# Low halves of a hybrid block's mixer weights: a negated copy on ScalarE and an accumulating transfer in place of a GpSimd subtraction

## The chip, the core and the metric

The kernel runs on one core of a Trainium2 chip. A core has five engines with a queue of instructions each: TensorE (PE, with its weight loads shown apart as PEld), VectorE (DVE), ScalarE (ACT), GpSimd (POOL) and SyncE (SP, which here only issues transfers). Each engine runs its own queue in order and waits for the others at semaphores. Tiles lie in on-chip memory with 128 partitions, sums of matmuls in banks of their own. The metric is the device time of one execution in microseconds (us), less being better.

## The reference

Two layers of a backbone over 256 latent tokens and 256 context tokens, width 1024, all in fp32. Every layer is a half-step SwiGLU, a token mixer with four branches, and another half-step SwiGLU. Of the mixer, what matters here is that everything starts from one wide projection and ends in merges:

```python
def token_mixer(h, hc, rope, p, ctx_out):
    (ca, cg, lx, lg, gqkv, gz, ga, gb, aq, ak, av, gates) = split_in(h @ p['w_in'])
    ...                                   # the same for the context: hc @ p['w_in']
    y_conv = conformer_conv(ca, cg, p)    # depthwise convolution, width 31
    y_lru, y_lru_c = rglru_branch(...)    # gated linear recurrence, both directions
    y_gdn, y_gdn_c = gdn_branch(...)      # chunked gated DeltaNet, both directions
    y_att = window_attention(...)
    def merge(y_a, y_b, y_c, y_d, gate_cols):
        gt = jax.nn.sigmoid(gate_cols).reshape(gate_cols.shape[:-1] + (N_BRANCH, D))
        mrg = gt[..., 0, :] * (y_a @ p['proj_conv'])
        ...                               # the three other branches likewise
        return mrg @ p['w_out']
```

In the second layer the context stream is needed only as far as the latent tokens read it, so most of its projections take 256 columns (tokens) and not 512.

## The kernel before

**Split products.** TensorE multiplies in a rounded 32-bit format (fp32r). To keep fp32 accuracy each operand is split into a rounded high half and a low half, the difference between the raw value and the high half, and `mm3` (lines 379 to 381) makes three products: high weights by high activations, high by low, low by high. All weights come from memory in pieces of 128 x 1024 (512 KB), called chunks here. One chunk feeds 24 matmuls where activations stand as 512 or 256 columns.

**A chunk** is made in `chunk` (line 98). SyncE loads it into a raw tile `wr` (two buffers), ScalarE writes the rounded half `wh` (line 120, three buffers, or a longer-lived slot F, Y, B or G), and DVE or GpSimd subtracts it from the raw tile into `wl` (line 121, three buffers). A raw buffer is free for the next load when that subtraction has read it.

**Which engine subtracts** is taken from the string `self.lo`, letter by letter, by the running number of the chunk: "D" is DVE, "P" GpSimd. The FFNs set "DDP" or "D". In the mixers a table `ORDER` holds one letter for each step of work; its capital letters P, D and X set `self.lo` by the table `LO` to "P", to "DP" (turn about) and to "D". After that table `mixer` sets "DP" in the first layer and "D" in the second, for the merges of two branches and the fetch of `wo` (the table `TAIL`, where an X sets "D").

**What sets the order.** A scheduler places the instructions on the engines by priority and by its own estimate of durations, so a change of one operation moves others. The transfers are issued by SyncE in one queue: a load that waits for its raw buffer holds up everything behind it, among it the loads `gt<-gsp` (lines 818 and 822) which feed the steps of the DeltaNet scan, and the stores `gsp<-G`.

**Other names that the prediction uses.** Line 1107 is the width-31 convolution on DVE: 240 multiply-adds `C<-C,vec`, each with two operands in on-chip memory. Lines 858 to 893 are the steps of the scan, which alternate between TensorE, DVE and GpSimd (line 868 decays the state). Line 1049 is the short convolution of the recurrence. Line 1294 adds a gated product into the merge tile on GpSimd. Line 132 loads an identity matrix at the start; it is the only transfer that GpSimd issues. `wab` is a small weight of 64 KB that ScalarE's queue loads.

Of the kernel before, what the change touches and what calls it, by code (L numbers as in the profile page):

```python
# [12 lines left out]
F32 = mybir.dt.float32  # L13
# [3 lines left out]
ALU = mybir.AluOpType  # L17
P = 128
D = 1024
# [13 lines left out]
    0, 124, 128, 132, 136, 168, 176, 184, 192, 200, 296, 298, 300, 301, 309)  # L33
NEG = -1e30
N_CH = 16
LO = {"P": "P", "D": "DP", "X": "D"}
ORDER = (
    "eggePgegeggXgeggggggPgegggvggvggvggvgggggggaabgggabggzabababzabababllllggababababzababgllablglzbvvvvvccccvvccvccssssssssPssssssDmmllllmmllllsmmmmsmmmmmmmm",
    "gPggggeeeggecgggcgeggggeggccgvgvggvvggggccgagggggbaabgzggggvggabzvabgccggvabbabazbvvvvvzssssslssssssslllllsPssmmlllllsmmmllllmlmmmmmmmmmm",
# [10 lines left out]
class Net:  # L50
# [46 lines left out]

    def chunk(self, src, at=None, raw=None):
        nc = self.nc
        pool_lo = self.lo[self.n_ck % len(self.lo)] == "P"  # L100
        self.n_ck += 1
        if raw is None:
            raw = self.sb.tile([P, 1024], F32, tag="wr", bufs=2, name="wr")
            nc.sync.dma_start(raw, src)
        elif isinstance(raw, str):
            raw = self.slot(raw, name="raw")[:, :1024]
            nc.sync.dma_start(raw, src)
        if at == "G":
            hi, lo = ([self.G(F32R) for _ in range(2)] for _ in range(2))
            parts = [(hi[k], lo[k], raw[:, k * 512:(k + 1) * 512]) for k in range(2)]  # L110
        else:
            if at:
                w = self.slot(at, F32R, name="w" + at)
                hi, lo = w[:, :1024], w[:, 1024:]
            else:
                hi = self.sb.tile([P, 1024], F32R, tag="wh", bufs=3, name="wh")
                lo = self.sb.tile([P, 1024], F32R, tag="wl", bufs=3, name="wl")
            parts = [(hi, lo, raw)]
        for h, l, r in parts:
            nc.scalar.copy(h, r)  # L120
            (nc.gpsimd if pool_lo else nc.vector).tensor_sub(l, r, h.bitcast(F32))  # L121
        return hi, lo

    def split(self, hi, lo, src, pool_lo=True):
# [280 lines left out]
    def ffn(self, l, f, j, tiles, H, fill, after, start=None):  # L405
# [9 lines left out]
        def two(src, at=(None, None)):  # L415
            if lat:
                return self.pair(src, "Y", at)
            return [chunk(src[a], at[a]) for a in range(2)]

        for fi, (m0, m1) in enumerate(F_SPLIT):  # L420
# [48 lines left out]
            if fi < len(F_SPLIT) - 1:  # L469
                for dh in range(2):  # L470
                    ps = {t: self.ps("px" if t == 3 else "pm") for t in tiles}
                    ws = []
                    for i in range(n):
                        i0 = m0 // 2 + i
                        if i == n - 1 and not i % 2:
                            ws.append(chunk(src[dh][i]))
                        elif not i % 2:
                            ws += two(self.t["f2"][l, f, dh, i0:i0 + 2])
                        w = ws[i]
                        for t in tiles:  # L480
                            self.down_mm(ps[t], hid, t, n, i, w)
                        if fill and i % 2:
                            fill.pop(0)()
                    for t in tiles:
                        self.resid(t, dh, ps[t], ALPHA if fi == 0 else 1.0)
            else:
                while fill:
                    fill.pop(0)()
                ws = [[chunk(src[dh][i], at=DOWN_AT[dh][i]) for i in range(n)] for dh in range(2)]


# [41 lines left out]
        else:  # L533
            nc.vector.tensor_add(x, x, t1)

# [1 line left out]

    def z_mm(self, ps, w, H, c):
        for k in range(KD):
# [759 lines left out]
    def mixer(self, l, H, last, after):  # L1299
        nc = self.nc  # L1300
        tiles = (2, 3) if last else (0, 1, 2, 3)
        c = slice(256, 512) if last else slice(0, 512)
        self.vec = self.sb.tile([P, V_N], F32, tag="vec", bufs=1, name="vec")
        with self.tc.issue_after(self.mark):
            nc.scalar.dma_start(self.vec, self.t["vec"][l])
        self.l, self.inv = l, None
        self.ysp = [self.dr.tile([P, 4, 512], F32, tag=f"ysp{b}", bufs=1, name="ysp") for b in range(4)]
        for s in range(2):
            if not (last and s == 0):
                nc.sync.dma_start(self.xspill[s], self.x[s])  # L1310
        self.z_head(l, H, [Z_GK + h for h in range(4)] + [Z_AK if last else Z_GQ])
        S, extra = self.att_z(l, H, last)
        self.conv_init()
        self.gdn_init()
        st = dict(
            g=self.gdn(l, H, last), v=self.gdn_values(l, H, last), s=self.gdn_scan(last),
            e=(f() for f in extra), a=self.att(self.att_scores, S, tiles),
            b=self.att(self.att_values, S, tiles), z=(self.gdn_z(l, H, last, h) for h in range(4)),
            c=(x for i in range(4) for x in self.conv(l, H, last, i)), l=self.lru(l, H, last), m=self.merges(l, H, last, c))
        ws = {}  # L1320
        self.emit(st, ORDER[l], "gvezabclsm")
        self.lo = "D" if last else "DP"
        y = [None, None]
        if last:
            mh = [a.rearrange("p (k t) -> p k t", k=KD) for a in (self.F(F32R), self.F(F32R))]
            spots = SPOT
        else:
            spots = ("F", "F", "F", "F", "F", "G", "G", None)
        self.ju = self.T

        def fetch(n0, n1):
            for n in range(n0, n1):
                ws[n] = self.chunk(self.t["wo"][l, n // 4, n % 4], at=spots[n])

        def conv_out():
            y[0] = self.new_y()
            self.conv_norm(last, y[0])
            yield

        def gdn_out():  # L1340
            y[1] = self.new_y()
            for t in tiles:
                self.gdn_out(t, y[1])
                yield

        done = [0] * 4

        def merged(i):
            done[i] += 1
            if last and done[i] == 2:  # L1350
                self.mh_split(mh, i, c)

        def merge_conv():
            for i in range(4):
                yield from self.merge(l, 0, y[0], H, last, False, i, lambda: merged(i))

        def merge_gdn():
            for i in range(4):
                yield from self.merge(l, 2, y[1], H, last, False, i, lambda: merged(i))

        def fetches():
            for i in range(4 if last else 7):
                fetch(i, i + 1)
                yield

        self.emit(dict(n=conv_out(), o=gdn_out(), c=merge_conv(), g=merge_gdn(), f=fetches()), TAIL[l], "nocgf")
        if not last:
            mh = self.new_h()
            for i in range(4):
                self.mh_split(mh, i, c)  # L1370
        self.x = [None, None]
        for s in range(2):
            if not (last and s == 0):
                self.x[s] = self.Y(name="x")
                nc.sync.dma_start(self.x[s], self.xspill[s])
        self.gate_rows(l, 1, 0.5, (1,) if last else (0, 1))
        self.norm_rows(l, 1)
        fetch(4 if last else 7, 8)

        def mm(t, dh, sums):  # L1380
            ps = self.ps()
            with self.hold():
                for i in range(4):
                    self.wo_mm(ps, mh, t - 2 if last else t, i, ws[4 * dh + i])
            self.resid(t, dh, ps, ALPHA, sums)

        self.out_loop(tiles, mm, after)

    def emit(self, streams, order, rest):
        for ch in order:  # L1390
            if ch in LO:
                self.lo = LO[ch]
            else:
# [165 lines left out]
```

## Time and profile before

| | us |
|---|---|
| median of 3 runs | 2820.98 (2819.75 to 2821.17) |
| span of the profiled execution | 2816.3 |
| PE busy | 2593.8 (92%) |
| DVE busy | 1955.0 (69%) |
| ACT busy | 1093.3 (39%) |
| POOL busy | 1008.0 (36%) |
| first mixer, about | 390 to 1200 |
| second mixer, about | 1945 to 2600 |

The profile is of one execution, and its times are counted from the start of its span. The span is 4.7 us less than the median of the runs; the profiled execution has no other time of its own. The two mixers were found by where the loads of `in_win` and `in_wo` stand. Matmuls are pipelined: one of 512 columns is shown with about 0.4 us, while the next starts some 0.22 us after it.

### The profile page before, as it was taken

How to read it: one execution, taken by the hardware profiler on the slowest of the kernel's cores; microseconds unless marked ns; L12 is line 12 of the kernel's file. 1: busy time of each engine (PE TensorE's matmuls, PEld its weight loads, DVE VectorE, ACT ScalarE, POOL GpSimd, SP SyncE). 2: the span in 40 equal slices, each digit the busy share in tenths (PEclk: the TensorE clock that was granted, in tenths of full speed). 3: DMA queues.
4: the chain of work that ended last, by engine and by line, in shares of the span. 5: the costliest groups of instructions: out<-in, count | busy, mean ns of one | idle time of the engine just before them, and what ended most of it. 6: DMA issues, size and time to landing. Idle time of an engine off the chain costs nothing.

```text
span 2816.3 us, 37869 instructions
## 1 busy us (share of the span) xinstructions
PE 2593.8 (92%) x14382; PEld 2174.2 (77%) x14382; DVE 1955.0 (69%) x3129; ACT 1093.3 (39%) x1995; POOL 1008.0 (36%) x691
## 2 busy tenths in 40 slices
PE   5999998998898999999999999999979878888898
PEld 3787877776777787878878888888867767688898
DVE  8695966678999834265969467623698898756455
ACT  3322235483332533353222442223536534344443
POOL 4323223222535344433232332323332278731221
PEclk9999999999999999999999999999989989999899
DMA  6554542234422343434545344423222534357353
GB/s 226 191 179 169 201 145 102 69 109 153 140 83 91 113 135 117 164 113 157 181 171 196 102 166 167 149 95 115 91 90 92 156 116 133 105 183 240 135 181 118
DMA packets 162216, 396.99 MB, mean 141 GB/s; under 512 B 28417, under 2 KB 68577, under 8 KB 161265
## 3 DMA queue, kind: packets, MB, share of 16 engines
q1 hardware_dynamic: 158114, 384.55, 40.9%
q10 hardware_dynamic: 3888, 9.96, 1.1%
q8 instruction: 113, 1.85, 0.3%
q14 instruction: 69, 0.57, 0.1%
q0 software_dynamic: 32, 0.07, 0.0%
HBM read 360.92 MB, written 33.60 MB: 140 GB/s over the span
## 4 chain that ended last, share of the span: by engine, by line
PE 34%; DVE 13%; issue 3%; DMA 2%; POOL 2%; ACT 2%; SPq 0%; POOLq 0%; ACTq 0%; DVEq 0%
PE pm L380 10%; PE pm L381 10%; PE pm L379 10%; DVE C L1107 2%; DVE G L572 1%; DVE junk L169 1%; DVE wl L121 1%; DVE G L864 1%; PE px L381 1%; PE px L380 1%; PE px L379 1%; DMA wr<-in_wo_dram 1%; DVE lru L1049 1%; DVE M L781 1%; PE pg L873 0%
## 5 line engine op out<-in xcount | busy, mean ns | idle before, releaser
L379 PE MATMUL pm<-h,wh 128*128 128x512 f32 (+1 forms) x2512 | 895.5, 358 | 36.6 <-ACT h L125 12.8
L381 PE MATMUL pm<-h,wl 128*128 128x512 f32 (+1 forms) x2512 | 890.9, 355 | 16.8 <-DVE wl L121 14.8
L380 PE MATMUL pm<-h,wh 128*128 128x512 f32 (+1 forms) x2512 | 892.0, 355 | 13.0 <-POOL h L127 6.7
L121 POOL TENSOR_TENSOR wl<-wr,wh 128x1024 fp32r<-128x1024 f32 x166 | 419.8, 2530 | 697.6 <-ACT wh L120 649.0
L120 ACT CAST wh<-wr 128x1024 fp32r<-128x1024 f32 x340 | 356.7, 1050 | 785.6 <-PE pm L380 275.2
L379 PEld LDWEIGHTS pm<-h,wh 128*128 128x128 f32 x2512 | 484.0, 193 | 109.1 <-ACT h L125 15.6
L381 PEld LDWEIGHTS pm<-h,wl 128*128 128x128 f32 x2512 | 484.8, 193 | 87.0 <-DVE wl L121 18.8
L380 PEld LDWEIGHTS pm<-h,wh 128*128 128x128 f32 x2512 | 485.1, 193 | 80.9 <-POOL h L127 10.1
L121 DVE TENSOR_TENSOR wl<-wr,wh 128x1024 fp32r<-128x1024 f32 x174 | 243.6, 1400 | 263.0 <-ACT wh L120 261.6
L169 DVE SCALAR_TENSOR_TENSOR junk<-wa,cb 128x1024 bf16<-128x1024 f32 x256 | 358.3, 1442 | 9.2 <-DMA wa<-in_adaw_dram 8.6
L127 POOL TENSOR_TENSOR F<-G,F 128x512 fp32r<-128x512 f32 (+1 forms) x94 | 139.4, 1483 | 426.2 <-ACT F L125 426.1
L1107 DVE SCALAR_TENSOR_TENSOR C<-C,vec 128x482 f32<-128x482 f32 (+29 forms) x240 | 208.2, 867 | 4.1 <-ACT C L1099 0.9
L380 PE MATMUL pm<-wl,F 128*128 128x512 f32 x368 | 145.5, 395 | 0.0
L379 PE MATMUL pm<-wh,F 128*128 128x512 f32 x368 | 145.4, 395 | 0.0
L381 PE MATMUL pm<-wh,F 128*128 128x512 f32 x368 | 144.1, 395 | 0.0
L393 DVE TENSOR_TENSOR G<-G,pm 128x512 f32<-128x512 f32 (+1 forms) x93 | 54.4, 585 | 125.9 <-PE pm L381 118.9
L121 DVE TENSOR_TENSOR wl<-raw,wh 128x1024 fp32r<-128x1024 f32 x61 | 75.0, 1231 | 63.6 <-ACT wh L120 63.6
L125 ACT CAST F<-G 128x512 fp32r<-128x512 f32 (+1 forms) x94 | 50.9, 542 | 154.1 <-DVE G L393 154.1
L868 POOL TENSOR_TENSOR wk<-wk,cd 128x512 f32<-128x512 f32 x56 | 70.8, 1267 | 94.1 <-PE pg L890 75.4
L572 DVE SCALAR_TENSOR_TENSOR G<-pm,vec,G 128x506 f32<-128x506 f32 (+5 forms) x126 | 87.2, 692 | 24.5 <-ACT G L567 22.7
L120 ACT CAST wh<-raw 128x1024 fp32r<-128x1024 f32 x64 | 66.8, 1047 | 88.1 <-PE pm L380 38.8
L1294 POOL TENSOR_TENSOR mrg<-mrg,M 128x512 f32<-128x512 f32 (+1 forms) x48 | 51.9, 1085 | 117.5 <-DVE M L1293 117.5
(408 smaller groups left out, 4493.8 us busy)
## 6 DMA issues: line engine op xcount, KB each, us to landing
wr<-in_f_dram SPq DMA_DIRECT2D x204, 512.0 KB, 3.6
wa<-in_adaw_dram SPq DMA_DIRECT2D x72, 1024.0 KB, 4.9
wr<-in_win_dram SPq DMA_DIRECT2D x132, 512.0 KB, 3.6
raw<-in_f_dram SPq DMA_DIRECT2D x30, 1024.0 KB, 4.9
wr<-in_prj_dram SPq DMA_DIRECT2D x32, 512.0 KB, 3.7
gt<-gsp SPq DMA_DIRECT2D x12, 768.0 KB, 5.2
gsp<-G SPq DMA_DIRECT2D x32, 256.0 KB, 2.7
wr<-in_wo_dram SPq DMA_DIRECT2D x16, 512.0 KB, 3.7
```

Source lines behind the costliest of these rows:

```text
L120: nc.scalar.copy(h, r)
L121: (nc.gpsimd if pool_lo else nc.vector).tensor_sub(l, r, h.bitcast(F32))
L127: eng.tensor_sub(lo, src, hi.bitcast(F32))
L169: nc.vector.scalar_tensor_tensor(junk, w3[:, a], 1.0, self.cb[:, s], op0=ALU.mult, op1=ALU.mult, accum_out=self.modT[l][:, i + a, s:s + 1])
L379: nc.tensor.matmul(ps, wh, xh, start=first, stop=False)
L380: nc.tensor.matmul(ps, wh, xl, start=False, stop=False)
L381: nc.tensor.matmul(ps, wl, xh, start=False, stop=last)
L393: nc.vector.tensor_mul(hf[:, c], sg[:, c], pu[:, c])
L572: nc.vector.scalar_tensor_tensor(acc[:, :, d:], src[:, :, :n - d], w(j), acc[:, :, d:], op0=ALU.mult, op1=ALU.add)
L868: nc.gpsimd.tensor_mul(S(d, n + 1).rearrange("p (h e) -> p h e", h=4), S(d, n).rearrange("p (h e) -> p h e", h=4), gs["cd"][:, d * N_CH + ...
L1107: V.scalar_tensor_tensor(o, x, w(j), o, op0=ALU.mult, op1=ALU.add)
L1294: nc.gpsimd.tensor_add(dst, dst, th[:, c])
```

## The change

In the mixers, what "P" did is done by a new kind "A": ScalarE writes the negated rounded half into the low tile, and GpSimd issues a transfer that adds the raw tile to it, from on-chip memory to on-chip memory. The tables say so: "P" in `ORDER` now gives "A", "D" gives "DA", and the tail of the first layer's mixer has "DA". The FFNs' "DDP" and the first stage's "P" stay with GpSimd's subtraction. In the built program 113 transfers of this kind stand on GpSimd, of 111 chunks (two chunks of the tail go in two halves), 56 in the first mixer and 57 in the second, and as many new instructions on ScalarE.

```diff
-LO = {"P": "P", "D": "DP", "X": "D"}
+LO = {"P": "A", "D": "DA", "X": "D"}
...
-        pool_lo = self.lo[self.n_ck % len(self.lo)] == "P"
+        kind = self.lo[self.n_ck % len(self.lo)]
...
         for h, l, r in parts:
             nc.scalar.copy(h, r)
-            (nc.gpsimd if pool_lo else nc.vector).tensor_sub(l, r, h.bitcast(F32))
+            if kind == "A":
+                nc.scalar.mul(l, h.bitcast(F32), -1.0)
+                nc.gpsimd.dma_start(l, r, accum_op=ALU.add)
+            else:
+                (nc.gpsimd if kind == "P" else nc.vector).tensor_sub(l, r, h.bitcast(F32))
...
-        self.lo = "D" if last else "DP"
+        self.lo = "D" if last else "DA"
```

The lines behind `chunk` move down by four in the changed file. Three places show what moved.

GpSimd, tail of the first layer's mixer (`mrg` is the merge tile, `wF` and `G` are long-lived slots for `wo`). Before:

```order
L121 TENSOR_TENSOR wl<-wr,wh 128x1024
L1294 TENSOR_TENSOR mrg<-mrg,M 128x512
L121 TENSOR_TENSOR wF<-wr,wF 128x1024
L1294 TENSOR_TENSOR mrg<-mrg,M 128x512
L121 TENSOR_TENSOR wl<-wr,wh 128x1024
L1294 TENSOR_TENSOR mrg<-mrg,M 128x512
L121 TENSOR_TENSOR G<-wr,G 128x512 x2
```

With the change:

```order
L123 DMA wl<-wr 128x1024
L1298 TENSOR_TENSOR mrg<-mrg,M 128x512
L123 DMA wF<-wr 128x1024
L1298 TENSOR_TENSOR mrg<-mrg,M 128x512
L123 DMA wl<-wr 128x1024
L123 DMA G<-wr 128x512 x2
```

Each subtraction has become the issue of a transfer, at nearly the same place between the merges' additions.

ScalarE, second layer's mixer, around the load of `wab` (`wh` is the rounded half, `C` the convolution's tile, `q` the queries). Before:

```order
L120 CAST wh<-wr 128x1024 x2
L1099 ACTIVATE C<-C,vec 128x256
L608 ACTIVATE G<-G 128x512
L567 ACTIVATE G<-px,vec 128x512
L1155 COPY q<-pm 128x256
L120 CAST wh<-wr 128x1024
L608 ACTIVATE G<-G 128x512
L619 DMA G<-in_wab_dram 128x128
```

With the change:

```order
L120 CAST wh<-wr 128x1024
L122 ACTIVATE wl<-wh 128x1024
L1103 ACTIVATE C<-C,vec 128x256
L612 ACTIVATE G<-G 128x512
L571 ACTIVATE G<-px,vec 128x512
L120 CAST wh<-wr 128x1024
L1159 COPY q<-pm 128x256
L122 ACTIVATE wl<-wh 128x1024
L612 ACTIVATE G<-G 128x512
L623 DMA G<-in_wab_dram 128x128
```

The new instruction stands right behind its cast or a few places later, behind work that waits for other engines.

SyncE, second layer's scan (`T<-ysp` and `gt<-gsp` are loads of the merges and of the scan). Before:

```order
L104 DMA wr<-in_win_dram 128x1024
L818 DMA gt<-gsp 128x2x768
L104 DMA wr<-in_win_dram 128x1024
L820 DMA G<-asp 128x512
L104 DMA wr<-in_win_dram 128x1024
L104 DMA wr<-in_prj_dram 128x1024
L1070 DMA ysp<-T 128x256
L818 DMA gt<-gsp 128x2x768
```

With the change:

```order
L104 DMA wr<-in_win_dram 128x1024
L822 DMA gt<-gsp 128x2x768
L824 DMA G<-asp 128x512
L104 DMA wr<-in_win_dram 128x1024
L1074 DMA ysp<-T 128x256
L104 DMA wr<-in_win_dram 128x1024
L822 DMA gt<-gsp 128x2x768
L104 DMA wr<-in_prj_dram 128x1024
```

The loads of chunks and of the scan keep nearly their order; a scan load still stands behind a chunk's load.

## Rows read from the trace of the kernel before

**Rows 1.** Page, part 1: busy us, share of the span, instructions, by engine
```profile
PE 2593.8 (92%) x14382; PEld 2174.2 (77%) x14382; DVE 1955.0 (69%) x3129; ACT 1093.3 (39%) x1995; POOL 1008.0 (36%) x691
```

**Rows 2.** Table by stretches (us): their length, then each engine's busy time
```profile
core 0: us, PE busy (x) PEld busy (x) DVE busy (x) ACT busy (x) POOL busy (x), PEclk, DMA share, GB/s
460.00:620.00 160.00, 149.91 (x809) 124.90 (x808) 107.21 (x224) 92.02 (x262) 42.23 (x21) 0.97 0.29 90
620.00:980.00 360.00, 324.28 (x2068) 256.73 (x2067) 316.27 (x522) 136.71 (x269) 152.92 (x134) 0.96 0.36 116
...
2060.00:2420.00 360.00, 296.42 (x2015) 255.15 (x2015) 320.74 (x574) 162.73 (x371) 196.06 (x148) 0.92 0.38 119
...
980.00:1200.00 220.00, 218.04 (x1005) 178.29 (x1004) 88.21 (x120) 78.19 (x127) 95.61 (x59) 1.00 0.41 134
```

**Rows 3.** Groups by line, 2060 to 2420, then 620 to 980: busy us, mean ns
```profile
L1107 DVE SCALAR_TENSOR_TENSOR C<-C,vec 128x241 f32<-128x241 f32 (+14 forms) x120 | 92.8, 773 | 1.8
...
L121 POOL TENSOR_TENSOR wl<-wr,wh 128x1024 fp32r<-128x1024 f32 x44 | 107.4, 2444 | 122.1 <-ACT wh L120 114.1 <-PE px L1213 6.8 <-PE pg L706 1.1
...
L1107 DVE SCALAR_TENSOR_TENSOR C<-C,vec 128x482 f32<-128x482 f32 (+14 forms) x120 | 115.4, 961 | 2.3 <-ACT C L1099 0.9
...
L121 POOL TENSOR_TENSOR wl<-wr,wh 128x1024 fp32r<-128x1024 f32 x19 | 46.9, 2470 | 61.0 <-ACT wh L120 31.7 <-PE px L1052 8.4 <-PE pg L706 7.6
```

**Rows 4.** Line 1107 in 2060 to 2420, then 620 to 980: ns min/median/max
```profile
L1107 DVE SCALAR_TENSOR_TENSOR C<-C,vec x120: 455/480/2655, 2068.0 to 2342.5; 128x241 f32<-128x241 f32 x8, 128x242 f32<-128x242 f32 x8, 128x243 f32<-128x243 f32 x8, 128x244 f32<-128x244 f32 x8
...
L1107 DVE SCALAR_TENSOR_TENSOR C<-C,vec x120: 704/734/2890, 718.3 to 948.5; 128x482 f32<-128x482 f32 x8, 128x484 f32<-128x484 f32 x8, 128x486 f32<-128x486 f32 x8, 128x488 f32<-128x488 f32 x8
```

**Rows 5.** Chain that ended last, 2068 to 2094: start us, us, what
```profile
2068.76 2.50 DVE C L1107
...
2078.44 2.51 DVE C L1107
...
2088.17 0.49 DVE C L1107
```

**Rows 6.** Transfers: KB each, median us from issue to landing; GpSimd's one issue
```profile
wr<-in_win_dram SPq DMA_DIRECT2D x132, 512.0 KB, 3.6
...
G<-in_wab_dram ACTq DMA_DIRECT2D x2, 64.0 KB, 2.7
...
ident<-in_ident_dram POOLq DMA_DIRECT2D x1, 64.0 KB, 5.3
...
L132 POOL DMA_DIRECT2D ident<-in_ident_dram x1: 735/735/735, 1.2 to 1.2; - x1
```

**Rows 7.** Page, part 5: the cast of a chunk; line 121's subtractions, ns min/median/max
```profile
L120 ACT CAST wh<-wr 128x1024 fp32r<-128x1024 f32 x340 | 356.7, 1050 | 785.6 <-PE pm L380 275.2
...
L121 DVE TENSOR_TENSOR wl<-wr,wh x174: 1190/1225/3368, 81.5 to 2795.0; 128x1024 fp32r<-128x1024 f32 x174
L121 POOL TENSOR_TENSOR wl<-wr,wh x166: 2335/2399/3387, 81.4 to 2486.3; 128x1024 fp32r<-128x1024 f32 x166
```

**Rows 8.** GpSimd in order of time, 1060 to 1182: start us, us, instruction
```profile
1063.18 2.39 POOL L121 TENSOR_TENSOR wl<-wr,wh 128x1024 fp32r<-128x1024 f32 x1 [3.28 <-ACT wh L120]
...
1116.12 2.39 POOL L121 TENSOR_TENSOR wl<-wr,wh 128x1024 fp32r<-128x1024 f32 x1 [7.75 <-ACT wh L120]
...
1179.12 2.54 POOL L121 TENSOR_TENSOR G<-wr,G 128x512 fp32r<-128x512 f32 x2 [1.31 <-ACT G L120]
```

**Rows 9.** SyncE in order of time, two stretches: chunk loads, start us, us
```profile
2058.25 36.06 SPq L104 DMA_DIRECT2D wr<-in_win_dram  x9
...
2464.70 0.33 SPq L104 DMA_DIRECT2D wr<-in_win_dram  x1
...
2489.16 0.35 SPq L104 DMA_DIRECT2D wr<-in_win_dram  x1
```

**Rows 10.** Waits of PE, then of SyncE, 1945 to 2600: us, times, longest
```profile
PE px L1241 <- ACT T L1221: 10.0, 3, 5.0
...
SPq L104 <- POOL wl L121: 243.7, 50, 21.2
```

## The prediction

> **What bounds the kernel now.** I read the shares of the page first, then the table by stretches, then the groups and the chain in the stretches that the table points to. TensorE is busy for 92% of the span [rows 1], but it is not the limit everywhere. The table [rows 2] separates three kinds of stretch in the mixers. In 980 to 1200, the tail of the first mixer, PE is busy for 218.0 of 220 us: it is the limit, and DVE rests. In 460 to 620 PE has 149.9 of 160, so even where DVE is at 67% PE idles 6%; I take that as what a mixer's dependences cost anyway. In 2060 to 2420 DVE has 320.7 of 360 and PE only 296.4, and 620 to 980 is alike but milder (316.3 and 324.3): there DVE sets the pace.
>
> Part of that DVE time is no work. In 2060 to 2420 the convolution's multiply-adds have a median of 480 ns, but a mean of 773 [rows 3, 4], with single ones of up to 2655 ns. The chain shows them: 2.50 and 2.51 us beside 0.49 [rows 5]. That is the length of GpSimd's subtraction of a chunk (2.44 us, 44 of them in the stretch [rows 3]): a DVE instruction with two operands in on-chip memory stands still while GpSimd subtracts. So the 107.4 us of these subtractions [rows 3] are on the path although GpSimd looks half idle.
>
> The second thing to see is the raw buffer. SyncE's loads of chunks waited 243.7 us in the second mixer for GpSimd's subtraction to free a raw buffer [rows 10], and the subtractions in the tail of the first mixer come as close as 63.0 us for eight pitches [rows 8], 7.9 us each. One buffer's round is a load of 3.6, a cast of 1.05 and the subtraction of 2.40 [rows 6, 7], 7.05 us. It is already near the pitch.
>
> **The change, part by part.** All sums are made against the profiled span of 2816.3 us; the median of the runs is 4.7 us above it, and the difference is put on the median.
>
> *DVE set free.* Removed are 111 subtractions of about 2.4 us on GpSimd. In 2060 to 2420 the line of the convolution alone loses 120 x (773 - 480) = 35 us of standing still [rows 3, 4]; the most that 44 subtractions can hold DVE is 107 us. I take 70, about the middle, since other two-operand groups stand in the same stretch; DVE then has some 250 us, less than PE's 296. So PE is next, and the gain is capped by PE's idle time: at the 6% of 460 to 620 [rows 2], 296.4 / 0.937 = 316 us, 44 less than now. In 620 to 980 the same cap is 324.3 / 0.937 = 346, 14 less; the convolution shows 120 x (961 - 734) = 27 us there. Whether the issue of a transfer also holds DVE is not shown; GpSimd's only issue took 0.735 us [rows 6], 30% of a subtraction. If it does, 30% stays. I take 70% of the caps, 31 and 10, together -41; the ends are -58 (all of it) and -20 (half of that taken). In the other stretches PE is already at 94 to 99%, and I take nothing.
>
> *ScalarE.* Added are 113 instructions; the cast of the same shape takes 1.05 us [rows 7], so at most 119 us. None of it would matter if ScalarE waited for nothing in order, but the negation stands between its cast and work that DVE waits for. In the four stretches of rows 2 ScalarE has 470 of 1100 us, so it has room. Its work grows by a quarter. PE's largest wait for it in the second mixer is 10.0 us [rows 10]; a quarter of that, twice for the smaller waits, and for two mixers, is about 6. The ends are 0 and 31. I take +6, nearer to the low end, since that one wait is the row that shows ScalarE on PE's path.
>
> *The raw buffer's round.* This is the term that decides. A raw tile is now held through the load (3.6), the cast (1.05), the negation (1.05) and the whole transfer that adds it, from issue to landing, L. No row shows L. From below, a plain load of 512 KB from the hardware queues takes 3.6; from above, GpSimd's only transfer took 5.3 for 64 KB [rows 6], and going from 64 to 512 KB costs 3.6 - 2.7 = 0.9 on the other queues, twice that if both operands have to be read: 7.1. I take 5.3 + 0.9 = 6.2, since the one row of the same queue is the nearest. The round is then 5.7 + 6.2 = 11.9 us in place of 7.05. The Trainium skill ("DMA: Bandwidth & Descriptors", section "Anatomy of one DMA — SWDGE (gpsimd) path") fits such a transfer as 2.0 us plus its bytes over 436 GB/s, 3.2 us for 512 KB; the row disagrees, with 5.3 where that fit gives 2.2 for 64 KB. By the page this term would all but vanish and the time would be about 2790.
>
> In the first mixer's tail the kinds alternate, and so do the two raw buffers: every "A" chunk has the same buffer, and a pair cannot go faster than its round. From 1063.18 to 1116.12 there are five pitches of 10.6, from 1116.12 to 1179.12 eight of 7.9 [rows 8]; at 11.9 they cost 5 x 1.3 + 8 x 4.0 = 38.5. Against that stand two chunks that are ready ahead, each 24 matmuls of 218.0 / 1005 = 0.217 us [rows 2], together 10.4. That leaves +28. PE is full there, so nothing else hides it.
>
> In the second mixer all chunks are "A" until the tail, both buffers have the round, and the pitch is at least 11.9 / 2 = 5.95. From 2058.25 on, nine loads take 36.06 us, eight pitches of 4.5, and from 2464.70 to 2489.16 there are five pitches of 4.9 [rows 9]: 8 x 1.5 + 5 x 1.05 = 17. Of it some is covered by chunks that are ready ahead; I take +15. Elsewhere the chunks come more slowly than 5.95 us and are hidden by the other engines' work; if the freed DVE asks for chunks faster, this cover goes, and the gain above stops at the buffer. Together +43; the ends are +2 (L 3.6) and +63 (L 7.1).
>
> *What is queued behind.* A chunk's load waits for the transfer to land, and SyncE's queue waits with it. Behind stand the scan's loads and stores: ten times a load of `gt` stands right behind a chunk's load in the new order. Each waits up to 11.9 - 7.05 = 4.85 us longer, but the scan loads one pair of steps ahead. I take 0.8 us for each, +8; the ends are 4 and 10 once most of it is hidden. On GpSimd itself the issue waits for ScalarE's negation, 1.05 us later than the subtraction did, and holds back the scan's decay and the merge's additions; it is shorter by 1.7 us, so I count nothing for it.
>
> Sum: -41 + 6 + 43 + 8 = +16, on the median 2837.
>
> **The rivals.** *Faster: the transfer is quick, and DVE's freedom is what is left.* For it speaks that the only transfer of GpSimd's queue ran at the program's start beside the loads of the inputs, so L may be far below 6.2. Each us of L is worth 13 in the tail (less what is ready ahead, so 10 or 11), some 6 in the second mixer and 2 in SyncE's queue, about 19 together. The sum is zero at L = 6.2 - 16 / 19, about 5.4: below it the kernel is faster. At 3.6 to 4.8 it comes to 2785 to 2810; I put it at 2795.
>
> *No change that can be measured.* The two large terms, -41 and +43, differ by less than either is known. Within 0.2% (5.6 us, about what a measurement of this kernel can tell from no change) is L between about 5.1 and 5.7: 2821.
>
> *Much slower: adding in a transfer costs far more than copying.* No row shows an accumulating transfer. If it reads both operands one after the other and its landing goes to 8 us or more, the tail's round is 13.7 and the second mixer's pitch 6.85: 1.8 us x 19 = 34 more, 2871 and up. For it speaks that DMA engines are already busy for 0.36 to 0.41 of these stretches [rows 2].
>
> *The change does not free DVE, and DVE holds up the transfers.* If the issue on GpSimd and DVE's instructions exclude each other as the subtraction did, each transfer starts up to a DVE instruction (0.7 us) later, 0.7 x 19 = 13 more, and half of the gain (15) goes too: 2865. The Trainium skill says so for a part of DVE's instructions ("SBUF — State Buffer", section "Who interferes with whom"): copies and one-operand instructions in a double-port mode keep GpSimd from writing a transfer's descriptors. Nothing in this trace shows it, and the convolution's lines are not of that kind.
>
> **How the numbers follow.** The forecast, a little slower by the raw buffer, 0.36: 2837, with 2827 to 2860 as its own range. Faster 0.32. No change 0.15. Much slower 0.12. DVE not freed 0.05. That gives faster 0.32, same 0.15, slower 0.53. The range reaches down to L = 3.6 with the whole of DVE's gain (-58 + 6 + 2 + 4 = -46, 2775) and up to L = 7.1 with the small gain and ScalarE at its high end short of a third (-20 + 20 + 63 + 10 = +73, 2894).
>
> **What would show it.** In the profile of the changed kernel, the landing of the transfers of line 123 against 6.2 us is the first thing to read; below 5.4 the faster rival holds. The convolution's lines should lose their 2.5 us pieces, with a mean near the median in 2060 to 2420, and DVE's busy time there should fall by some 70 us; if not, the last rival holds. In the tail of the first mixer TensorE should lose its 99%, with waits for the low tile and transfers 11 to 12 us apart; if it stays full, the buffer term is wrong. SyncE's waits of line 104 should be for landings of line 123. The forecast is wrong if the tail keeps its 220 us, or if the scheduler's new order moves the scan or the merges by more than these terms, which no row of before can tell.

## The result, and the profile after

The changed kernel takes 2891.28 us (median of runs from 2886.76 to 2893.58), the kernel before beside it 2820.36: a ratio of 1.0243, with a 95% interval from 1.0229 to 1.0258. It is slower by 71 us, where +16 was forecast. The sign held, the range (2775 to 2894) by 3 us; the size did not. The profiled execution has a span of 2888.5 us.

First the page: part 1 (busy time by engine), two groups of part 5, and two transfers of part 6.

```profile
PE 2634.9 (91%) x14382; PEld 2202.7 (76%) x14382; DVE 1820.2 (63%) x3129; ACT 1199.1 (42%) x2108; POOL 818.2 (28%) x691
...
L123 POOL DMA_DIRECT2D wl<-wr x106 | 93.3, 881 | 487.4 <-ACT wl L122 280.1
...
L122 ACT ACTIVATE wl<-wh 128x1024 fp32r<-128x1024 f32 x106 | 112.0, 1057 | 1.1
...
wr<-in_win_dram SPq DMA_DIRECT2D x132, 512.0 KB, 4.0
wl<-wr POOLq DMA_DIRECT2D x106, 512.0 KB, 5.4
```

Against [rows 1], DVE's busy time has fallen by 135 us and GpSimd's by 190, ScalarE has gained 106: the change does what it says. An adding transfer lands 5.4 us after its issue on the median, less than the 6.2 taken. And yet the time has gone up. The stretches that answer to [rows 2], matched by the number of matmuls that have started, show where:

```profile
core 0: us, PE busy (x) PEld busy (x) DVE busy (x) ACT busy (x) POOL busy (x), PEclk, DMA share, GB/s
458.00:616.00 158.00, 148.68 (x809) 123.45 (x809) 94.76 (x223) 105.23 (x277) 20.57 (x21) 0.98 0.54 140
616.00:979.00 363.00, 324.61 (x2068) 257.62 (x2068) 279.15 (x525) 156.41 (x290) 123.66 (x135) 0.95 0.51 143
2113.00:2482.00 369.00, 306.09 (x2003) 264.09 (x2006) 257.84 (x575) 201.68 (x411) 109.59 (x144) 0.88 0.70 173
979.00:1238.00 259.00, 235.52 (x1001) 184.67 (x1001) 78.57 (x116) 97.46 (x149) 60.59 (x57) 0.93 0.60 158
```

The tail of the first mixer has 259 us in place of 220, with TensorE at 91% in place of 99%. Of these 39 us 22 are idle time of TensorE; for the other 17 it is busy, with as many matmuls as before but at a granted clock of 0.93 in place of 1.00. So it is in the whole run: 14382 matmuls keep it busy 41 us longer than in [rows 1], at a mean granted clock of 0.953 (before 0.970). The middle of the second mixer has 369 in place of 360, though DVE's busy time there fell by 63: now neither DVE (70%) nor TensorE (83%) is full. Such a stretch is bound by a chain that goes from engine to engine, and the chain that ended last shows it. From 2123 to 2157 (start us, us, what):

```profile
2123.21 6.54 DMA wl<-wr
...
2129.82 3.98 DMA wr<-in_win_dram
...
2133.83 1.05 ACT wh L120
...
2134.91 1.07 ACT wl L122
...
2136.26 6.84 DMA wl<-wr
...
2143.15 4.16 DMA wr<-in_win_dram
...
2147.38 2.77 issue
...
2150.17 7.00 DMA wl<-wr
```

That is the raw buffer's round, over and over: the adding transfer lands, the next load starts, then cast, negation and the next transfer. 13.05 us pass from 2123.21 to 2136.26 and 13.9 to 2150.17. SyncE's waits from 1995 to 2680 us, which answer to the last of [rows 10] (in total, times, longest):

```profile
SPq L104 <- DMA wl<-wr: 332.3, 50, 24.1
```

By the loads that mark a mixer's begin and end (the load of `vec`, the last load of `norm_g` in it), the first mixer took 905.0 us (before 866.2), the feed-forward layers between 704.5 (696.0), the second mixer 677.3 (653.3), the rest 209.8 (210.2).

The 8 us between the mixers do not come from a wait for a chunk's low half. TensorE's order differs at the layer's start: the eight instructions of line 269 (now 273) stand behind some 140 products there, where they stood behind some 70. In the third ten us TensorE now stands idle for 2.8 us and then works at the lower of its two levels (1.2 and 2.4 GHz) for a part of the time, a granted clock of 0.69 on the mean:

```profile
1317.00:1327.00 10.00, 7.22 (x39) 6.69 (x38) 2.01 (x5) 3.17 (x7) 3.22 (x3) 0.69 0.00 0
```

The same ten us of the kernel before:

```profile
1277.00:1287.00 10.00, 10.00 (x86) 10.00 (x85) 2.07 (x3) 3.09 (x5) 2.98 (x2) 1.00 0.19 54
```

### The profile page after: what moved, and what is told of

The parts are those of the page before. It is cut to its first block, busy times and chain, and to the rows that moved or that the text cites. A ratio compares the mean times of both kernels' runs of the same rounds, so it can differ in the third digit from the quotient of the medians.

```text
span 2888.5 us, 38180 instructions
## 1 busy us (share of the span) xinstructions
PE 2634.9 (91%) x14382; PEld 2202.7 (76%) x14382; DVE 1820.2 (63%) x3129; ACT 1199.1 (42%) x2108; POOL 818.2 (28%) x691
## 3 DMA queue, kind: packets, MB, share of 16 engines
q8 instruction: 113, 1.85, 0.3%
## 4 chain that ended last, share of the span: by engine, by line
PE 36%; DMA 8%; DVE 5%; issue 4%; ACT 2%; POOL 1%; SPq 0%; POOLq 0%; ACTq 0%; DVEq 0%
PE pm L385 10%; PE pm L384 10%; PE pm L383 10%; DMA wl<-wr 3%; DMA wr<-in_win_dram 3%; DVE junk L173 1%; PE px L385 1%; PE px L384 1%; PE px L383 1%; DVE wl L125 1%; POOL h L131 0%; ACT wh L120 0%; DMA wr<-in_wo_dram 0%; DVE x L532 0%; PE pg L877 0%
## 5 line engine op out<-in xcount | busy, mean ns | idle before, releaser
L383 PE MATMUL pm<-h,wh 128*128 128x512 f32 (+1 forms) x2512 | 909.2, 364 | 63.2 <-ACT wh L120 23.4
L385 PE MATMUL pm<-h,wl 128*128 128x512 f32 (+1 forms) x2512 | 904.1, 361 | 36.0 <-DMA wl<-wr 20.8
L384 PE MATMUL pm<-h,wh 128*128 128x512 f32 (+1 forms) x2512 | 903.3, 360 | 12.4 <-DVE h L131 6.3
L383 PEld LDWEIGHTS pm<-h,wh 128*128 128x128 f32 x2512 | 495.8, 198 | 141.2 <-ACT wh L120 29.8
L385 PEld LDWEIGHTS pm<-h,wl 128*128 128x128 f32 x2512 | 496.0, 198 | 112.0 <-DMA wl<-wr 26.0
L384 PEld LDWEIGHTS pm<-h,wh 128*128 128x128 f32 x2512 | 495.9, 197 | 80.6 <-POOL h L131 10.0
L125 POOL TENSOR_TENSOR wl<-wr,wh 128x1024 fp32r<-128x1024 f32 x60 | 160.8, 2679 | 346.8 <-ACT wh L120 346.8
L123 POOL DMA_DIRECT2D wl<-wr x106 | 93.3, 881 | 487.4 <-ACT wl L122 280.1
L1111 DVE SCALAR_TENSOR_TENSOR C<-C,vec 128x482 f32<-128x482 f32 (+29 forms) x240 | 162.9, 679 | 7.9 <-ACT C L1103 4.9
L122 ACT ACTIVATE wl<-wh 128x1024 fp32r<-128x1024 f32 x106 | 112.0, 1057 | 1.1
```

The lines of the kernel that those rows point to most:

```text
L122: nc.scalar.mul(l, h.bitcast(F32), -1.0)
L123: nc.gpsimd.dma_start(l, r, accum_op=ALU.add)
L125: (nc.gpsimd if kind == "P" else nc.vector).tensor_sub(l, r, h.bitcast(F32))
L383: nc.tensor.matmul(ps, wh, xh, start=first, stop=False)
L384: nc.tensor.matmul(ps, wh, xl, start=False, stop=False)
L385: nc.tensor.matmul(ps, wl, xh, start=False, stop=last)
```

## The experiments

**Theory 1**, from the chain: the raw buffer's round is the loss. **Rivals**: the DMA engines are too full (theory 2), or ScalarE's queue with its 113 negations (theory 3). Each kernel was timed beside the kernel before, which took 2820 to 2824 us; ratios with 95% intervals.

**All transfers from DRAM.** The raw tile is then free after its cast, and all else stays (`s` is the chunk in DRAM).

```
-                nc.gpsimd.dma_start(l, r, accum_op=ALU.add)
+                nc.gpsimd.dma_start(l, s, accum_op=ALU.add)
```

> The accumulating transfer reads the chunk from DRAM a second time instead of from the raw tile, so that the raw tile is free after its cast (load 4.0 + cast 1.05 us); ScalarE's negation, the transfers' number and their landing in the low tile stay. Theory 1, the raw buffer's round: in the changed kernel's chain of waits of the second mixer a landing of 6.2 to 7.0 us and a load of 4.0 to 5.3 take turns, and SyncE's loads waited 602 us for these landings. Without that round the +27 us of the first mixer's tail and the some +24 of the second mixer go, and what DVE's freedom is worth (up to 41 us) shows: 2780 to 2825, with SyncE's waits for the landings gone. Theory 2, the DMA engines are too full (share 0.69 to 0.73 in the second mixer, 0.37 to 0.39 before) and every transfer is slower for it: the traffic stays, and the time stays at 2875 or above. Theory 3, ScalarE's queue with the negations: nothing of it changes, 2870 or above.

2820.52 us, ratio 0.9992 (0.9977 to 1.0008): all 71 us are gone. The transfers land even later (median 6.1 us), with as much traffic. SyncE's loads now wait for the cast (whole run):

```profile
SPq L104 <- ACT wh L120: 292.0, 66, 22.3
```

This rules out that traffic or ScalarE alone make the loss, since both are unchanged. But DVE's gain doesn't show either: something else takes it.

**Copying instead of adding.**

```
-                nc.gpsimd.dma_start(l, r, accum_op=ALU.add)
+                nc.gpsimd.dma_start(l, r.bitcast(F32R))
```

> The transfer copies the raw tile over the low tile instead of adding it (the low half is then the raw weight: the subtraction is left out). Everything else, ScalarE's negation and the wait for it included, stays. If adding is what makes the landing long (median 6.5 us in the second mixer's first part, 4.2 for the loads beside it), a copy lands in about 4 us, the round shortens by some 2.5 us, and at some 19 to 30 rounds on the path the time is 2815 to 2845. If a transfer of GpSimd's queue is as long without adding, the time stays within 6 us of the changed kernel's 2891.

2802.61 us, ratio 0.993 (0.9908 to 0.9953), 89 us less than with the addition. Line 123 (ns min/median/max; then us to landing):

```profile
L123 POOL DMA_DIRECT2D wl<-wr x106: 527/556/730, 486.2 to 2481.2; - x106
...
DMA to landing us min/median/max: 2.4/3.1/7.3
```

So adding makes the issue 0.31 us and the landing 2.3 us longer (0.87 and 5.4 in the changed kernel). That it was worth 89 us was more than any theory had; 2815 to 2845 was expected.

**Negation, and GpSimd adds by an instruction.**

```
-                nc.gpsimd.dma_start(l, r, accum_op=ALU.add)
+                nc.gpsimd.tensor_add(l, r, l.bitcast(F32))
```

> ScalarE's negation stays, and GpSimd adds the raw tile to it by an instruction instead of issuing a transfer. The kernel is then the one before with 113 ScalarE instructions of 1.06 us and a raw buffer held that much longer (8.1 us in place of 7.05). Theory 3, ScalarE's queue carries the loss: most of the 71 us stays, 2870 or above. Theory 1, the raw buffer's round: about 1.1 us for each of some 19 to 30 rounds, 2835 to 2855 at most. Theory 2, the transfers' traffic: it is gone, and only ScalarE's few us are left, 2821 to 2830.

2855.48 us, ratio 1.0111 (1.0086 to 1.0137), at the upper end of theory 1's band: 33 us for a step of 1.06 that lies on the round and on ScalarE both. By itself it can't tell the two apart.

**The transfers in the second mixer only.**

```
-                self.lo = LO[ch]
+                self.lo = LO[ch] if self.l else LO[ch].replace("A", "P")
...
-        self.lo = "D" if last else "DA"
+        self.lo = "D" if last else "DP"
```

> Only the second mixer uses transfers; the first one's chunks go to GpSimd's subtraction as before. By the loads' times, the changed kernel lost 40 us in the first mixer, 8 in the feed-forward layers behind it and 24 in the second mixer. If the losses simply stand side by side, the time is 2845 (2835 to 2855). If it is near 2821, the second mixer's loss was passed on from the first; if it is above 2860, the first mixer's is passed on to nothing.

2838.43 us, ratio 1.0065 (1.0039 to 1.0091). In its profile the second mixer takes 670.5 (+17), and the first one and the layers between are within some 3 us of before. The losses stand side by side.

**The transfers in the first mixer's tail only.** Here too the other chunks go to GpSimd's subtraction.

```
+        if kind == "A" and not 110 < self.n_ck <= 160:
+            kind = "P"
```

> The changed kernel's transfers only in the tail of the first mixer (110 < n_ck <= 160); all other chunks as before. The loads of the changed kernel came 28 to 35 us later through this stretch, the forecast took 28. If the tail's loss is its own: 2845 to 2858 (with the some 7 us at the start of the feed-forward layer behind, where TensorE ran at the lower clock). If it is the sum of what came before it: 2830 or less.

2860.72 us, ratio 1.0142 (1.0107 to 1.0177): +37, the tail's own (in its profile the first mixer takes 43 us longer, the layers behind it 4). In the changed kernel's tail GpSimd starts the transfers at

```profile
1153.13 0.87 POOL L123 DMA_DIRECT2D wl<-wr  x1 [6.13 <-ACT wl L122]
...
1164.98 0.87 POOL L123 DMA_DIRECT2D wl<-wr  x1
...
1174.21 0.87 POOL L123 DMA_DIRECT2D wF<-wr  x1 [3.42 <-ACT wF L122]
...
1184.21 0.87 POOL L123 DMA_DIRECT2D wl<-wr  x1 [5.42 <-ACT wl L122]
```

11.9, 9.2 and 10.0 us apart, where [rows 8] had 7.9. TensorE's waits from 1060 to 1239 name the cast, not the transfer:

```profile
PE pm L383 <- ACT wh L120: 11.7, 8, 3.7
PE pg L383 <- ACT wh L120: 8.4, 3, 7.3
...
PE pm L385 <- DMA wl<-wr: 0.2, 1, 0.2
```

A buffer that comes free late shows at the *next* chunk: its load is late, so its high half is. Whoever looks for the transfer among TensorE's waits finds 0.2 us here (22.7 in the whole run).

**Holding the raw buffer in the kernel before, first try.** A small transfer behind each of GpSimd's subtractions in the mixers, reading the raw tile.

```
+                scr = self.dr.tile([P, 256], F32, tag="scr", bufs=8, name="scr")
+                nc.gpsimd.dma_start(scr, r[:, :256])
```

> The kernel before, and behind each of GpSimd's subtractions in the mixers a transfer of a quarter of the raw tile (128 KB) from GpSimd's queue to a scratch tensor that nobody reads. It holds the raw buffer some 4 us longer (an issue of 0.6 to 0.9 and a landing of 2.4 to 3.1 by the plain copies), without an instruction on ScalarE, without a later low half, with little traffic. Theory 1, the raw buffer's round: the loss comes where the changed kernel lost, in the tail of the first mixer (the last 24 of its loads) and at the start of the second one (its first 16 loads), 15 to 40 us in all, 2836 to 2861. If the raw buffer is no limit: within 6 us of the kernel before.

2864.36 us, ratio 1.0152 (1.0127 to 1.0177), but not by the mechanism that was meant. The transfer only reads, so the scheduler put it ahead of the subtraction, and GpSimd's queue waited in it for loads:

```profile
L124 POOL DMA_DIRECT2D scr<-wr x115: 539/559/612, 457.6 to 2542.5; - x115
its engine sat idle before it (us, times) until:
  DMA wr<-in_win_dram: 185.7, 55
```

SyncE's loads waited for landings of these transfers too:

```profile
SPq L104 <- DMA scr<-wr: 178.3, 46, 6.7
```

So the 41 us can be the round's or those of GpSimd's queue; this run can't tell the two apart.

**The same, tied to the subtraction's result.** The transfer goes from the low tile into the dead raw tile.

```
+                nc.gpsimd.dma_start(r[:, :256].bitcast(F32R), l[:, :256])
```

> The transfers of the earlier hold kernel read only the raw tile, so the scheduler put them ahead of the subtraction, where they hold nothing back but GpSimd's queue. Here the small transfer (128 KB) goes from the low tile, which the subtraction has just written, into the dead raw tile, so it comes behind the subtraction and the next load of that buffer waits for its landing: some 3 us more for a round of 7.05, and no work on ScalarE. Theory 1, the raw buffer's round: at the 19 to 25 us for each us of round that the forecast and the copying kernel give, 30 to 75 us, 2850 to 2895, with a loss in the first mixer's tail (last 24 loads) and at the second mixer's start. If the raw buffer's round is not what the changed kernel lost: 2820 to 2835.

2894.87 us, ratio 1.0258 (1.0231 to 1.0285): +71, as much as the whole change, without a negation, without a low tile that comes later, and with a quarter of the bytes. Page part 6, and SyncE's waits in the whole run:

```profile
wr<-wl POOLq DMA_DIRECT2D x107, 128.0 KB, 2.0
...
SPq L104 <- DMA wr<-wl: 469.2, 79, 27.8
```

It holds the buffer 2.0 us longer, and as long as GpSimd's queue takes to come to it. GpSimd also spends some 65 us on issues here (115 of 0.57), so not every us need be the buffer's. By mixers the loss lies where the changed kernel's does: the first one takes 902.8 us (905.0 there). Within it the places differ: by matmuls started, 14 of its loss come before the tail and 22 in it, against none and 40 in the changed kernel.

**The transfers only for 40 chunks in the middle of the second mixer**, from the raw tile, then from DRAM, then none (subtracted on DVE), then every second one on DVE.

```
+        if kind == "A" and not 310 < self.n_ck <= 350:
+            kind = "P"
```

The second of these also has the line of the first experiment; the third and the fourth set the kind of the 40 by one more line each:

```
+        if kind == "A":
+            kind = "D"
...
+        if kind == "A":
+            kind = "AD"[self.n_ck % 2]
```

> The changed kernel's transfers from the raw tile only for the 40 chunks in the middle of the second mixer, all others as before. From DRAM the same 40 gave 2804.3 (19 us less than before). If the raw buffer has slack there (the chunks come 8.5 us apart on the mean, two rounds side by side 6.2), this is alike: 2800 to 2810. If the round limits there too, as the chain of waits of the changed kernel has it from 2110 to 2160: 2820 or above.

> The transfers, reading from DRAM, only for 40 chunks in the middle of the second mixer (310 < n_ck <= 350), where DVE sets the pace; all others as before, with GpSimd's subtraction. In the kernel with all transfers from DRAM, the loads of this stretch came 27 to 33 us earlier against those of the kernel before, and the tail behind gave 21 back. If the gain stands by itself: 2787 to 2800. If what the tail gave back belongs to the gain (the work behind is limited by something else): 2810 to 2822.

> The same 40 chunks, but their low halves subtracted on DVE (1.2 us each) instead of on GpSimd, and no transfer anywhere. If each of GpSimd's 2.4 us subtractions stops DVE for most of its length, DVE wins some (2.4 - 1.2) us for each of up to 40 chunks, at most 48 us of DVE's time, and the time falls by 10 to 30 us, 2790 to 2810. If GpSimd's subtractions stop it for less than half of their length, DVE loses: 2822 or above.

> The 40 chunks in the middle of the second mixer take turns: one by a transfer from DRAM, one subtracted on DVE; all others as before. All by transfers from DRAM gave 2804.3, all on DVE 2811.5, all on GpSimd 2823. If the transfers' traffic and ScalarE's negations hold the first of these back and DVE's work the second: 2785 to 2800. If GpSimd's subtraction being gone is all that counts: 2803 to 2812.

From the raw tile 2828.86 us (1.0015, 0.9999 to 1.0031: no change), from DRAM 2804.27 (0.9937, 0.9913 to 0.996), on DVE 2811.52 (0.995, 0.9933 to 0.9966), mixed 2810.71 (0.9956, 0.994 to 0.9971). In the one stretch where DVE sets the pace, the source of the transfer, and with it the hold of the raw buffer, makes 25 us of difference (22 by the ratios). That is more than there is to gain. The kernel from DRAM beats both kernels, by 18.8 us against the one before beside it. The times from DRAM and on DVE lie between the two ranges expected of each. That the mixture is no better than DVE alone fits the expectation that only GpSimd's missing subtraction counts; why, no run shows.

**ScalarE's negation by itself.** First no negation ahead of the copy; then both copying kernels with the copy from DRAM, where the raw buffer is free after the cast; then GpSimd negates, with adding transfers from DRAM.

```
-                nc.scalar.mul(l, h.bitcast(F32), -1.0)
```

> The copying transfer without ScalarE's negation ahead of it (the subtraction and the negation are left out; the low half is the raw weight): DVE is free of GpSimd's subtractions, ScalarE has its old work, and the transfer may start with the cast. It shows what ScalarE's 113 negations and the wait for them cost beside the copying kernel's 2803. If ScalarE's term is the some 6 us of the forecast: 2790 to 2798. If the negations are the larger part of the 33 us that negation and addition cost together: 2765 to 2780.

> As the kernel with all transfers from DRAM (2820.5), but the transfer copies instead of adding (the subtraction is left out; the negation is still made and waited for). The raw buffer is free after its cast in both. So the difference is what the longer landing of an adding transfer costs by itself, by the later low tile and the fuller DMA engines. If the raw buffer's round was all that the landing did in the changed kernel: within 8 us of 2820. If the later low tile counts as well: 2775 to 2805.

> The same without ScalarE's negation (subtraction and negation are left out). The raw buffer is free after its cast in both, so the difference to the kernel above is what ScalarE's 113 negations cost without any hold of the raw buffer. If the 46 us between the two copying kernels from the raw tile were ScalarE's own: again 30 to 50 us. If they were the raw buffer's round: 15 us or less.

```
-                nc.scalar.mul(l, h.bitcast(F32), -1.0)
+                nc.gpsimd.tensor_scalar_mul(l, h.bitcast(F32), -1.0)
```

> As the kernel with all transfers from DRAM (2820.5), but GpSimd makes the negation, so ScalarE has its old work, in time and in order; transfers and raw buffer as there. If ScalarE's negations carry the 46 us that the copying kernel gained without them: 2775 to 2795. If an instruction of GpSimd with one operand stops DVE as the subtraction does, and is as long: 2821 or above.

Medians in us; the last column is what the hold of the raw buffer costs, less what the later landing from DRAM costs:

| low half by | from the raw tile | from DRAM | difference |
|---|---|---|---|
| copy, no negation | 2756.71 | 2754.03 | 2.7 |
| copy behind the negation | 2802.61 | 2782.08 | 20.5 |
| addition behind the negation | 2891.28 | 2820.52 | 70.8 |

The ratios of the three that were not given yet: 0.977 (0.9748 to 0.9793), 0.9761 (0.9739 to 0.9783) and 0.9855 (0.9836 to 0.9875). The 2.7 is within the intervals. Copying without the negation is faster than the 2765 to 2780 expected. Down the column from DRAM, where no buffer is held, the negation costs 28 us (30 to 50 would have made it ScalarE's own, 15 the raw buffer's), and adding instead of copying 38. In the copying kernels TensorE multiplies raw weights in place of low halves; that this leaves its time alone is assumed. The late low tile shows in TensorE's waits for it: in the kernel that copies from DRAM

```profile
PE pm L385 <- DMA wl<-in_win_dram: 7.7, 7, 2.6
```

and in the one that adds from DRAM

```profile
PE pm L385 <- DMA wl<-in_win_dram: 24.2, 16, 4.1
```

Another part is TensorE's clock. Page part 1 of the three kernels from DRAM, in the order of the table:

```profile
PE 2581.3 (94%) x14382; PEld 2163.8 (79%) x14382; DVE 1813.9 (66%) x3129; ACT 1095.0 (40%) x1995; POOL 789.9 (29%) x691
...
PE 2594.6 (93%) x14382; PEld 2178.4 (78%) x14382; DVE 1828.0 (66%) x3129; ACT 1197.8 (43%) x2108; POOL 787.7 (28%) x691
...
PE 2611.8 (93%) x14382; PEld 2190.4 (78%) x14382; DVE 1832.6 (65%) x3129; ACT 1197.0 (42%) x2108; POOL 819.7 (29%) x691
```

From these to the changed kernel the profiled spans are 2753.3, 2780.0, 2822.0 and 2888.5 us, and TensorE's busy time makes 13, 17 and 23 us of the three steps, with the same number of matmuls, at mean granted clocks of 0.974, 0.969, 0.963 and 0.953. So by the profile a third to a half of each cost is not a wait but matmuls that take longer. That the waits bring the clock down is what the ten us from 1317 suggest; no run separates the two.

The negation does more than add 1.06 us. What GpSimd waited for ahead of its transfers (us, times), without it and with it:

```profile
  PE pm L384: 343.1, 65
...
  ACT wl L122: 247.3, 47
```

Without the negation a transfer needs neither load nor cast, only a low tile that TensorE has left. From 2110 to 2330 it starts 0.4 us after the start of the nearest cast on the median, with the negation 2.6 us. How the 28 divide between ScalarE's time and the low tile that comes later, these runs don't separate. GpSimd's negation didn't help (2872.74 us, 1.0176, 1.0145 to 1.0207): line 122 (ns min/median/max) is longer there than the subtraction that the change removed.

```profile
L122 POOL TENSOR_SCALAR wl<-wh x106: 2757/2771/4192, 483.5 to 2536.1; 128x1024 fp32r<-128x1024 f32 x106
```

## Why the prediction was right in sign and wrong in size

Along the table, from the kernel before to the changed one: 2822 to 2754 (subtractions gone from GpSimd and DVE free, neither negation nor addition paid), to 2782 (negation), to 2820 (adding), to 2891 (holding the raw buffer). Other orders of the steps would divide the sum a little differently. Term by term:

- **DVE set free: forecast -41, measured up to -68** (by the profiles 19 in the first mixer and 52 in the second, some given back between them; the -68 has a raw buffer in it that is free sooner). The mechanism held. The convolution in 2113 to 2482, against the mean of 773 and the 92.8 us of [rows 3]:

```profile
L1111 DVE SCALAR_TENSOR_TENSOR C<-C,vec 128x241 f32<-128x241 f32 (+14 forms) x120 | 67.2, 560 | 6.6 <-ACT C L1103 4.6
...
L1111 DVE SCALAR_TENSOR_TENSOR C<-C,vec x120: 454/474/4143, 2123.4 to 2400.0; 128x241 f32<-128x241 f32 x8, 128x242 f32<-128x242 f32 x8, 128x243 f32<-128x243 f32 x8, 128x244 f32<-128x244 f32 x8
```

  The nine of these instructions over 0.7 us all stand beside GpSimd's other two-operand instructions; none stood still for a transfer's issue alone, though ten of the 25 issues between 2110 and 2323 fall beside one. The 30% that I left for the issue, and the rival in which DVE isn't freed, fall. DVE's busy time fell by 63, where some 70 were said.
- **ScalarE: forecast +6, measured +28** with no buffer held. The step that failed is to scale one wait of TensorE (10.0 us, [rows 10]) by ScalarE's work; a quarter of it, twice, for two mixers, is 10 besides, and not 6. The negation lies on every chunk's way to its low half, and no row of waits for ScalarE lists that.
- **Adding against copying: no term, measured +38.** L stood in the sum only as a hold of the buffer. A low tile that lands later is also a low tile that TensorE waits for, raw buffer or not. To put this at nothing is the largest single miss.
- **The raw buffer and SyncE's queue: forecast +51, measured +71.** L was nearly right (6.2 taken; 5.4 on the median, 6.5 in 2110 to 2323), and so was the round (11.9 taken; 4.0 + 1.05 + 1.07 + 0.3 + 5.4 = 11.8). The tail came out at +37 for the 28 taken; of the 39 that it makes in the changed kernel's profile, 17 go with the lower clock, for which the sum has no term. Its eight short pitches went from 7.9 to 10.7 us on the mean, not to 11.9. The premise that every "A" chunk there has the same buffer doesn't hold throughout: the chunk whose transfer starts at 1153.13 was loaded from 1145.09 on, 1.2 us after the transfer before it had started, and none landed within 3.7. What failed in the second mixer is the cover: "elsewhere the chunks come more slowly than 5.95 us and are hidden by the other engines' work". The mean pitch in 2110 to 2323 is indeed 8.5 us (25 transfers in 213), but the chunks come in bursts, and the chain shows round behind round. Cover was reckoned from a mean. It should have been reckoned from the bursts: from 2019 to 2088, the start of the second mixer, (times of the kernel before) the loads fell another 28 us behind and the matmuls 15, and from 2420 to 2500 the matmuls another 15, where 17, less some cover, were taken for a part of both together. From 2088 to 2420, which was taken as covered, the matmuls gain 22 us in the kernel that adds from DRAM and 1 in the changed one.

Of the 55 us between forecast and measurement the missing term makes 38, ScalarE 22 and the buffer 20; the larger gain of DVE takes 27 back (the rest is that the kernels stood beside different runs of the one before). So the sign is the sum of four terms that were all too small. That the time lies in the range is luck: its upper end was made of L = 7.1 and a gain of 20, and neither came.

The test named to be read first misled: L came out at 5.4, the forecast's own point of no change, and the loss was 71. A threshold in one term is only as good as the other terms. Of the rest of what was named: SyncE's waits for landings, TensorE's lost 99% and the loss of most of the convolution's long pieces came true; the spacing of 11 to 12 us did so in part, and TensorE's waits for the low tile in the tail did not, they were for the cast. The rival "much slower" had the better time with the wrong mechanism: adding does cost more than copying, but L never had to reach 8 us.

On the page that the forecast weighed, the Trainium skill ("DMA: Bandwidth & Descriptors", section "Anatomy of one DMA — SWDGE (gpsimd) path"): its fit of 3.2 us for 512 KB agrees with the copying transfer on chip behind the negation, 3.1 us here, less with the one without it, 3.8, or from DRAM, 4.7, and my row of 5.3 us for 64 KB at the program's start was no guide to it. It is 2.2 us short for an adding one. The time of some 2790 that it would have given is near the 2802.61 of the copying kernel, but by chance, since the sum lacked 22 us of ScalarE's term and had 27 too little of DVE's.

## What to carry to other kernels

When an edit makes a buffer's reader slower, cost the whole round of the buffer, and reckon the cover from the shortest distances between its uses, not from their mean; here some two to five us more on a round of seven cost 71. Work that is taken off a busy engine should not go to a chain that holds the input longer: reading the input a second time from DRAM cost traffic and gave the 71 us back. A low tile that comes later is a cost of its own, and in these traces more idle time of TensorE came with a lower granted clock, which cost about as much again. Use the exchange only where the relieved engine sets the pace; in the 40 chunks where DVE did, it gained 19 us with the transfers from DRAM, and nothing with those from the raw tile.

## What the hardware showed unexpectedly

- From GpSimd's queue an adding transfer of 512 KB takes 5.4 us to land and 0.87 to issue, a copying one 3.1 and 0.56. From DRAM it is 6.1 and 4.7.
- GpSimd's negation, one operand, took 2.77 us for 128x1024, its subtraction of two 2.40. Beside a negation of 2.77 us in the second mixer DVE's convolution steps took up to 1.36 us in place of 0.47: they stood still for under 1 us, not for the whole of it. The longest of all, 1.85 us, stood beside one of 3.10.
- A change that touches no feed-forward layer moved one by 8 us, with another order at its start, a gap of 2.8 us on TensorE and a granted clock of 0.69 around it.
